# A GLA/S5 decoder step: norm temporaries in PSUM, sums of squares on VectorE, an earlier column sum

## The chip, the core and the metric

The kernel runs on one core of a Trainium2 chip. Its engines are called PE (TensorE, the matrix array; PEld is its weight load), DVE (VectorE), ACT (ScalarE), POOL (GpSimd) and SP (SyncE, which here issues the DMAs). Each runs its own queue in order, and semaphores make one wait for another. Operands lie in SBUF; PE writes PSUM, which has eight banks of 128x512 fp32 and which DVE and ACT can read and write too. The metric is the device time of one execution in microseconds (us).

## What is computed

Two layers of a decoder over 512 prompt tokens and 32 sample tokens with 1024 features: gated linear attention (GLA) and its MLP, then an S5 state-space mixer with a gated output (GLU) and its MLP. Each of the four sub-layers is wrapped in two root-mean-square norms, and the change concerns those around the sub-layers:

```python
def _rmsnorm(x, g):
    xf = x.astype(jnp.float32)
    y = xf * lax.rsqrt(jnp.mean(xf * xf, axis=-1, keepdims=True) + EPS)
    return (y * g.astype(jnp.float32)).astype(x.dtype)
...
    for i in range(DEPTH):
        h = _rmsnorm(x, prm['g_pre_mix'][i])
        ...                                # m = GLA or S5 mixer of h
        x = x + _rmsnorm(m, prm['g_post_mix'][i])
        h = _rmsnorm(x, prm['g_pre_mlp'][i])
        f = jnp.square(jax.nn.relu(h @ prm['w_up'][i])) @ prm['w_down'][i]
        x = x + _rmsnorm(f, prm['g_post_mlp'][i])
```

## The kernel before

**Tiles and jobs.** Features lie on the partitions, in `KD` = 8 blocks of 128; the 544 tokens lie along the free dimension in two halves, hf 0 of 288 and hf 1 of 256 (`HALF`). Each fp32 matmul is made of three: activations and weights are split into a high part (`xh`, `wh`, type fp32r) and what is left (`xl`, `wl`). A *job* is one 128-wide tile of outputs for one half: 8 blocks times 3 matmuls into one PSUM bank (`job`, `advance`), then `finish` copies it out (the "evac"). `PLAN` lists the jobs: groups of 4 or of 8 weight tiles, first all their jobs of half 0, then of half 1. The S5 input has an order of its own: five jobs of half 0, five of half 1, then in turn.

**Order.** There is no scheduler: instructions stand on each queue as the Python code emits them. `finish` runs, after job j's copy-out, the functions in `after[j]`; `defer(n, f)` appends f to the list n jobs ahead; `before_evac[j]` runs just ahead of job j's copy-out. `split_w` puts the weight split of later tiles between jobs: ACT casts `wh` (L113), DVE or POOL subtracts to get `wl` (L118, L120). While `dve_win` is 0, which `post` sets around the norms, POOL makes all of `wl`.

**The norms around a boundary.** At the end of a sub-layer the tiles of its output `acc` are finished one by one. `m_done` squares each on ACT into `sq` and adds it on DVE into `S1[hf]`. After the eighth, `post` defers: one job later `start` asks PE for the column sum of `S1` (a matmul with ones, `col_sums`, L243) and takes the root `r` (`rsqrt`: ACT makes an approximate root y, L251, and a scaled copy v of the sum, L252; DVE refines y in three instructions, L253 to L255). Then `step`, a few jobs in a row, walks the eight blocks: DVE scales `acc` by g and r (L318), adds it to the residual `X` (L320) and, for the next sub-layer, `xh` = X times its g (`pre_hi`: L278 on DVE for half 0, L280 on ACT for half 1), the square on ACT, its add into `S2[hf]` on POOL (L264 is the line of all these adds), and `xl` on DVE (`pre_lo`, L290). The first jobs of the next sub-layer need `xh` and `xl`; the copy-out of its first job needs `pre_scale`: the column sum of `S2`, and a root from it, `rs`. The last norm of the kernel is `last_done`. `SL` is the number of jobs over which each half's steps go.

Where the next sub-layer starts with a group of 8 tiles, half 1's eight jobs lie between half 0's last job and half 0's next one. So PE meets, in this order: those eight jobs; the next sub-layer's first job (it needs all of half 0's `xh` and `xl`); the column sum of `S2[0]`; the column sum of `S1[1]`, asked for by half 1's `start`; the second job.

**Banks.** PSUM's banks are two pools of four, `ps` and `held`. While `apart` is false, every request (`bank`) takes from the two in turn, so that jobs and small sums share all eight; while it is true, jobs take from `held` and everything else from `ps`. Before, it is true only from within the S5 input to the first third of the GLU.

Of the kernel before, what the change touches and what calls it, by code (L numbers as in the profile page):

```python
# [46 lines left out]
SL = (4,6)  # L47
# [25 lines left out]
class Builder:  # L73
    def __init__(self, tc, io):
        self.tc, self.nc, self.io = tc, tc.nc, io
        self.jobs = 0
        self.after = defaultdict(list)
        self.before_evac = defaultdict(list)
        self.hold, self.held = set(), []
# [166 lines left out]
    def rsqrt(self, ps, n, scale, out):  # L246
        nc = self.nc
        y = self.p_t.tile([128, 288], F32, tag="ny", name="ny", bufs=1)
        a = self.p_t.tile([128, 288], F32, tag="na", name="na", bufs=1)
        v, y, a = out, y[:, :n], a[:, :n]  # L250
        nc.scalar.activation(y, ps, AF.Abs_reciprocal_sqrt, scale=scale, bias=self.vec[:, V_EPS:V_EPS + 1])  # L251
        nc.scalar.activation(v, ps, AF.Copy, scale=scale, bias=EPS)  # L252
        nc.vector.tensor_mul(a, y, y)  # L253
        nc.vector.scalar_tensor_tensor(a, a, -0.5, v, op0=OP.mult, op1=OP.mult)
        nc.vector.scalar_tensor_tensor(out, a, 1.5, y, op0=OP.add, op1=OP.mult)  # L255

    def square_into(self, s, src, n, first, eng=None, later=False):
        nc = self.nc
        if first:
            nc.scalar.activation(s, src, AF.Square)  # L260
            return
        q = self.p_t.tile([128, 288], F32, tag="sq", name="sq", bufs=5)
        nc.scalar.activation(q[:, :n], src, AF.Square)
        add = lambda: (eng or nc.gpsimd).tensor_tensor(s, s, q[:, :n], op=OP.add)  # L264
        if later:
            self.defer(1, add)
        else:
            add()

    def pre_hi(self, hf, k, g, on_dve=False, later=False, squares=None):  # L270
# [30 lines left out]
    def post(self, hf, g_post, g_pre, sink=None):  # L301
# [10 lines left out]

        def step(ks):
            new = [k for k in ks if k < KD]
            xs, ms = ([t[:, k, c0:c1] for k in new] for t in (self.X, self.acc))
            for k, m in zip(new, ms):
                gk = self.vec[:, g_post + k:g_post + k + 1]
                nc.vector.scalar_tensor_tensor(m, m, gk, R["r"][:, :n], op0=OP.mult, op1=OP.mult)  # L318
            for x, m in zip(xs, ms):
                nc.vector.tensor_add(x, x, m)  # L320
            if g_pre is not None and ks[0]:
                self.pre_lo(hf, ks[0] - 1, g_pre)
            for k in new:
                if g_pre is not None:
                    self.pre_hi(hf, k, g_pre, hf == 0, True)
                if sink:
# [10 lines left out]
        self.defer(lead, start)  # L337
# [4 lines left out]
        ks = list(range(KD + 1))  # L342
# [49 lines left out]
    def m_done(self, m, hf, g_post, g_next, sink=None):  # L392
# [8 lines left out]
        if m == KD - 1:  # L401
            self.post(hf, g_post, g_next, sink)
# [181 lines left out]
    def gla_out(self, og):  # L584
        nc = self.nc

        def out_evac(m, hf, ps):
            c0, c1 = HALF[hf]
            nc.scalar.activation(self.acc[:, m, c0:c1], ps, AF.Copy)
            self.m_done(m, hf, V_POST, V_MPRE)  # L590
        self.run_block(og["h"], og["l"], out_evac)
# [516 lines left out]
    def s5(self, ctx):  # L1108
# [202 lines left out]
        OB = 6  # L1311
        self.after[self.jobs + OB].append(lambda: setattr(self, 'apart', True))
# [23 lines left out]
    def glu(self, zh, zl):  # L1336
# [15 lines left out]
        for q in (0, 4, 8):  # L1352
            self.run_block(zh, zl, lambda i, hf, ps: glu(i, q, hf, ps))
            if q == 0:
                self.apart = False


    def run(self):
        nc, tc, io = self.nc, self.tc, self.io
        ctx = ExitStack()  # L1360
        with ctx:
# [9 lines left out]
            self.vec = p.tile([128, V_END], F32, name="vec")  # L1371
            self.X = p.tile([128, KD, NT], F32, name="X")
# [156 lines left out]
```

## Time and profile before

| | |
|---|---|
| median of 3 runs | 1358.02 us (1356.08 to 1359.86) |
| the profiled execution | 1359.06 us, its span 1357.3 us |
| granted PE clock, mean | 0.978 |
| busy: PE / PEld / DVE / ACT / POOL | 1298.1 / 1270.3 / 798.9 / 602.4 / 509.9 us |
| HBM | 128.17 MB read, 25.46 MB written |

The span is from the first to the last instruction on the chip; the time of an execution is 1.8 us longer. Rows of the profile name instructions by line, engine, operation and tiles as out<-in, with partitions x elements; for groups there follow the total and the mean of one in ns. In square brackets stands the engine's idle time ahead of an instruction, and what ended it. `mm` and `held` are banks of jobs. Matmuls overlap in the array, so that one shows as longer than its distance to the next.

### The profile page before, as it was taken

Reading aid. Unit: us, or ns where it says so; the run is one execution under the profiler, and the core shown is the slowest. Engines: PE = TensorE matmul, PEld = TensorE weight load, DVE = VectorE, ACT = ScalarE, POOL = GpSimd, SP = SyncE. Lnnn points to the kernel's source line nnn. Section 1 sums busy time; section 2 is a strip of 40 time slices with the busy share of each in tenths; the row PEclk is TensorE's granted clock in tenths of the full one; section 3 lists DMA queues with packets and bytes.
Section 4 is the critical chain, followed back from the end, with each engine's and each line's share of the span. In section 5 each row is a group of like instructions: output and inputs, shape, how many; then the busy total and the mean of one; then the engine's idle time right before and its main releaser. Section 6 shows DMA issues by size and latency. Waiting matters only on the chain. (4 is left out here: it accounts for less than half of the span.)

```text
span 1357.3 us, 25681 instructions
## 1 busy us (share of the span) xinstructions
PE 1298.1 (96%) x9966; PEld 1270.3 (94%) x9966; DVE 798.9 (59%) x1779; ACT 602.4 (44%) x1349; POOL 509.9 (38%) x644
## 2 busy tenths in 40 slices
PE   7999999979999999999998988999899999999996
PEld 6899999979999999999997988999899999999996
DVE  7866564688535767666468689456841332332346
ACT  6633354645435646555434222434643432432432
POOL 4443244564381111121435443544633333343341
PEclk9999899999999999999998989999899999999998
DMA  6233222322325555544315687341222323222221
GB/s 190 94 128 102 104 68 86 121 65 75 98 71 161 174 162 172 164 149 152 109 47 187 176 254 222 96 125 35 91 78 74 99 79 109 78 81 91 78 63 67
DMA packets 80683, 155.31 MB, mean 114 GB/s; under 512 B 9040, under 2 KB 45264, under 8 KB 79536
## 3 DMA queue, kind: packets, MB, share of 16 engines
q1 hardware_dynamic: 80560, 153.66, 36.3%
q8 instruction: 78, 1.28, 0.4%
q14 instruction: 45, 0.37, 0.1%
HBM read 128.17 MB, written 25.46 MB: 113 GB/s over the span
## 5 line engine op out<-in xcount | busy, mean ns | idle before, releaser
L120 POOL TENSOR_TENSOR wl<-raw,wh 128x384 fp32r<-128x384 f32 (+3 forms) x351 | 351.9, 1014 | 597.8 <-ACT wh L113 588.9
L113 ACT ACTIVATE wh<-raw 128x512 fp32r<-128x512 f32 x368 | 219.6, 621 | 125.9 <-PE held L191 76.4
L118 DVE TENSOR_TENSOR wl<-raw,wh 128x128 fp32r<-128x128 f32 (+3 forms) x324 | 180.4, 568 | 102.6 <-ACT wh L113 96.6
L191 PE MATMUL held<-xh,wh 128*128 128x256 f32 (+1 forms) x792 | 235.1, 297 | 0.1
L191 PE MATMUL held<-xl,wh 128*128 128x256 f32 (+1 forms) x792 | 232.2, 293 | 0.8 <-DVE xl L290 0.8
L191 PE MATMUL held<-xh,wl 128*128 128x256 f32 (+1 forms) x792 | 230.9, 292 | 0.0
L191 PE MATMUL mm<-xl,wh 128*128 128x288 f32 (+1 forms) x744 | 216.7, 291 | 1.8 <-DVE xl L290 1.8
L191 PE MATMUL mm<-xh,wh 128*128 128x288 f32 (+1 forms) x744 | 218.2, 293 | 0.0
L191 PE MATMUL mm<-xh,wl 128*128 128x288 f32 (+1 forms) x744 | 215.1, 289 | 0.0
L191 PEld LDWEIGHTS held<-xh,wh 128*128 128x128 f32 x792 | 152.5, 193 | 1.6 <-issue 0.8
L191 PEld LDWEIGHTS held<-xl,wh 128*128 128x128 f32 x792 | 152.3, 192 | 1.4 <-DVE xl L290 1.0
L191 PEld LDWEIGHTS held<-xh,wl 128*128 128x128 f32 x792 | 152.0, 192 | 0.0
L191 PE MATMUL mm<-hh,wl 128*128 128x256 f32 (+1 forms) x512 | 147.5, 288 | 0.7 <-DVE wl L118 0.7
L191 PE MATMUL mm<-hl,wh 128*128 128x256 f32 (+1 forms) x512 | 148.1, 289 | 0.0
L191 PE MATMUL mm<-hh,wh 128*128 128x256 f32 (+1 forms) x512 | 148.1, 289 | 0.0
L191 PE MATMUL held<-hl,wh 128*128 128x256 f32 (+1 forms) x512 | 148.1, 289 | 0.0
L191 PE MATMUL held<-hh,wh 128*128 128x256 f32 (+1 forms) x512 | 148.0, 289 | 0.0
L191 PE MATMUL held<-hh,wl 128*128 128x256 f32 (+1 forms) x512 | 147.4, 288 | 0.0
L191 PEld LDWEIGHTS mm<-xl,wh 128*128 128x128 f32 x744 | 141.7, 190 | 3.2 <-DVE xl L290 3.0
L191 PEld LDWEIGHTS mm<-xh,wh 128*128 128x128 f32 x744 | 142.0, 191 | 1.3 <-issue 0.6
L191 PEld LDWEIGHTS mm<-xh,wl 128*128 128x128 f32 x744 | 141.3, 190 | 0.0
L363 ACT ACTIVATE r<-r 128x256 f32<-128x256 f32 (+1 forms) x128 | 55.0, 429 | 172.0 <-DVE r L361 171.9
(401 smaller groups left out, 2729.2 us busy)
## 6 DMA issues: line engine op xcount, KB each, us to landing
raw<-in_w SPq DMA_DIRECT2D x184, 512.0 KB, 3.6
S<-in_h SPq DMA_DIRECT2D x4, 1024.0 KB, 5.0
out_gla_s<-S SPq DMA_DIRECT2D x4, 1024.0 KB, 3.9
wd<-blk SPq DMA_DIRECT2D x16, 256.0 KB, 2.7
wd<-cs SPq DMA_DIRECT2D x16, 256.0 KB, 3.8
qd<-blk SPq DMA_DIRECT2D x16, 256.0 KB, 2.7
qt<-qd SPq DMA_DIRECT2D x16, 256.0 KB, 3.9
wt<-wd SPq DMA_DIRECT2D x12, 256.0 KB, 4.3
```

The costliest lines, as they stand in the source:

```text
L113: nc.scalar.activation(h[:, a:c], r[:, a:c], AF.Copy)
L118: nc.vector.tensor_sub(l[:, a:b], r[:, a:b], f32(h[:, a:b]))
L120: nc.gpsimd.tensor_sub(l[:, b:c], r[:, b:c], f32(h[:, b:c]))
L191: self.nc.tensor.matmul(ps[:, :c1 - c0], a[:, k], b[:, k, c0:c1], start=(k == 0 and i == 0), stop=(k == KD - 1 and i == 2))
L363: nc.scalar.activation(r[:, :n], r[:, :n], AF.Square)
```

## The change

- In `job`, functions in a new table `mid` are emitted ahead of a job's last block (the last 3 of its 24 matmuls). `post` puts half 0's `start` there, in the job behind the last one; half 1's stays behind that job.
- `m_done` issues, behind the last square, an ACT instruction of one column with the root's function (`spare`), so that its table is loaded there.
- `rsqrt`: y lies in a PSUM bank, and the first two DVE instructions change places of y and v, so that each of the three has one operand in PSUM.
- `step`: the product acc g r goes into a PSUM bank (`xm`) instead of back into `acc`; `xh` is always made on ACT; the square of X goes into the same bank. `xl` of a step's blocks follows in the next step, the last in a step of its own. The eight blocks go over 5 jobs instead of 4 for half 0 (`SL`), 6 as before for half 1; at the S5 input there are only 4.
- `square_into`: squares go into banks (`sq`), all adds are on DVE, and deferred ones are put at the head of the next job's list, so that they come before its step, the youngest first.
- `apart` is true from `gla_out` to the end.

```diff
-SL = (4,6)
+SL = (5,6)
...
+        if self.jobs in self.mid:
+            self.advance(t, hf, hi, lo, KD - 1)
+            for f in self.mid.pop(self.jobs):
+                f()
         self.advance(t, hf, hi, lo, KD)
...
     def rsqrt(self, ps, n, scale, out):
-        y = self.p_t.tile([128, 288], F32, tag="ny", name="ny", bufs=1)
+        y = self.bank("ny") if self.apart else self.p_t.tile([128, 288], F32, tag="ny", name="ny", bufs=1)
...
-        nc.vector.tensor_mul(a, y, y)
-        nc.vector.scalar_tensor_tensor(a, a, -0.5, v, op0=OP.mult, op1=OP.mult)
+        nc.vector.tensor_mul(a, y, v)
+        nc.vector.scalar_tensor_tensor(a, a, -0.5, y, op0=OP.mult, op1=OP.mult)
         nc.vector.scalar_tensor_tensor(out, a, 1.5, y, op0=OP.add, op1=OP.mult)
...
+        if q is None:
+            q = self.squares(n)
+        nc.scalar.activation(q, src, AF.Square)
+        add = lambda: (nc.vector if self.apart else eng or nc.gpsimd).tensor_tensor(s, s, q, op=OP.add)
         if later:
-            self.defer(1, add)
+            self.after[self.jobs + 1].insert(0, add)
...
+    def squares(self, n):
+        if self.apart:
+            return self.bank("sq")[:, :n]
+        return self.p_t.tile([128, 288], F32, tag="sq", name="sq", bufs=5)[:, :n]
...
         def step(ks):
+            ms = [self.bank("xm")[:, :n] for k in ks]
+            for k, m in zip(ks, ms):
                 gk = self.vec[:, g_post + k:g_post + k + 1]
-                nc.vector.scalar_tensor_tensor(m, m, gk, R["r"][:, :n], op0=OP.mult, op1=OP.mult)
+                nc.vector.scalar_tensor_tensor(m, self.acc[:, k, c0:c1], gk, R["r"][:, :n], op0=OP.mult, op1=OP.mult)
+            for k, m in zip(ks, ms):
+                x = self.X[:, k, c0:c1]
                 nc.vector.tensor_add(x, x, m)
+            if g_pre is not None:
+                for k in fresh:
+                    self.pre_lo(hf, k, g_pre)
+                fresh[:] = ks
+                for k, m in zip(ks, ms):
+                    self.pre_hi(hf, k, g_pre, False, True, None, m)
...
-        self.defer(lead, start)
+        if hf:
+            self.defer(lead, start)
+        else:
+            self.mid[self.jobs + 1].append(start)
...
-            part = ks[i * 9 // slots:(i + 1) * 9 // slots]
+            part = list(range(KD))[i * KD // slots:(i + 1) * KD // slots]
             self.defer(lead + i, lambda part=part: step(part))
+        self.defer(lead + slots, lambda: step([]))
...
         if m == KD - 1:
+            self.nc.scalar.activation(self.spare, self.vec[:, V_EPS:V_EPS + 1], AF.Abs_reciprocal_sqrt)
             self.post(hf, g_post, g_next, sink)
...
+        self.apart = True
         self.run_block(og["h"], og["l"], out_evac)
...
-        OB = 6
-        self.after[self.jobs + OB].append(lambda: setattr(self, 'apart', True))
...
-            if q == 0:
-                self.apart = False
```

How this moves the queues is shown at three places. Tile numbers shift by one (`S_80` and `S_81` before, `S1` of the two halves, are `S_81` and `S_82` now; `S_83` now is `S2` of half 0, `S_84` of half 1), and lines move by up to 18 (L318 is L330 now, L320 L333, L290 L301, L264 L270).

ACT at the end of gla_out's first half, from the last block's copy and square, before:

```order
L589 ACTIVATE acc<-mm 128x288
L263 ACTIVATE sq<-acc 128x288
L113 ACTIVATE wh<-raw 128x512
L589 ACTIVATE acc<-held 128x256
L260 ACTIVATE S_81<-acc 128x256
L251 ACT_TABLE_LOAD
```

and now:

```order
L606 ACTIVATE acc<-held 128x288
L269 ACTIVATE sq<-acc 128x288
L418 ACT_TABLE_LOAD
L418 ACTIVATE spare<-vec 128x1
L114 ACTIVATE wh<-raw 128x512
L256 ACTIVATE ny<-sums,vec 128x288
L257 ACTIVATE rp<-sums 128x288
L606 ACTIVATE acc<-held 128x256
L265 ACTIVATE S_82<-acc 128x256
```

The table load moved behind the square, and the root ahead of the next job's copy and square.

DVE at the same boundary, from the last instruction of the root, before:

```order
L255 SCALAR_TENSOR_TENSOR rp<-na,ny 128x288
L318 SCALAR_TENSOR_TENSOR acc<-acc,vec,rp 128x288 x2
L320 TENSOR_TENSOR X<-X,acc 128x288 x2
L278 TENSOR_SCALAR xh<-X,vec 128x288 x2
L290 SCALAR_TENSOR_TENSOR xl<-X,vec,xh 128x288
L318 SCALAR_TENSOR_TENSOR acc<-acc,vec,rp 128x288 x2
L320 TENSOR_TENSOR X<-X,acc 128x288 x2
L290 SCALAR_TENSOR_TENSOR xl<-X,vec,xh 128x288
```

and now:

```order
L260 SCALAR_TENSOR_TENSOR rp<-na,ny 128x288
L330 SCALAR_TENSOR_TENSOR xm<-acc,vec,rp 128x288
L333 TENSOR_TENSOR X<-X,xm 128x288
L330 SCALAR_TENSOR_TENSOR xm<-acc,vec,rp 128x288 x2
L333 TENSOR_TENSOR X<-X,xm 128x288 x2
L301 SCALAR_TENSOR_TENSOR xl<-X,vec,xh 128x288
L270 TENSOR_TENSOR S_83<-S_83,xm 128x288 x2
L270 TENSOR_TENSOR S_82<-S_82,sq 128x256
L330 SCALAR_TENSOR_TENSOR xm<-acc,vec,rp 128x288
L333 TENSOR_TENSOR X<-X,xm 128x288
L301 SCALAR_TENSOR_TENSOR xl<-X,vec,xh 128x288 x2
```

`xh` has left the queue, and the adds of the squares, of which S2's were on POOL and six of S1's stood behind all steps, stand between the steps.

DVE at the S5 input, half 1, from the last step to the root of the first job of half 1 (`us` is the copy-out of the fifth job of half 0), before:

```order
L318 SCALAR_TENSOR_TENSOR acc<-acc,vec,rp 128x256 x2
L320 TENSOR_TENSOR X<-X,acc 128x256 x2
L290 SCALAR_TENSOR_TENSOR xl<-X,vec,xh 128x256 x3
L1168 TENSOR_TENSOR us<-held,rs_84 128x72x4
L253 TENSOR_TENSOR na<-ny 128x256
```

and now:

```order
L330 SCALAR_TENSOR_TENSOR xm<-acc,vec,rp 128x256 x2
L333 TENSOR_TENSOR X<-X,xm 128x256 x2
L301 SCALAR_TENSOR_TENSOR xl<-X,vec,xh 128x256 x2
L1186 TENSOR_TENSOR us<-held,rs_85 128x72x4
L270 TENSOR_TENSOR S_84<-S_84,xm 128x256 x2
L301 SCALAR_TENSOR_TENSOR xl<-X,vec,xh 128x256 x2
L258 TENSOR_TENSOR na<-ny,rs_86 128x256
```

The last two `xl` moved behind the copy-out of the fifth job, with two adds ahead of them.

More of the change, by code (lines that the diff above doesn't have):

```diff
@@ L78, in __init__ @@
         self.before_evac = defaultdict(list)
+        self.mid = defaultdict(list)
         self.hold, self.held = set(), []
@@ L252, in rsqrt, with square_into @@
         nc.scalar.activation(v, ps, AF.Copy, scale=scale, bias=EPS)
-        nc.vector.tensor_mul(a, y, y)
-        nc.vector.scalar_tensor_tensor(a, a, -0.5, v, op0=OP.mult, op1=OP.mult)
+        nc.vector.tensor_mul(a, y, v)
+        nc.vector.scalar_tensor_tensor(a, a, -0.5, y, op0=OP.mult, op1=OP.mult)
         nc.vector.scalar_tensor_tensor(out, a, 1.5, y, op0=OP.add, op1=OP.mult)
-    def square_into(self, s, src, n, first, eng=None, later=False):
+    def square_into(self, s, src, n, first, eng=None, later=False, q=None):
         nc = self.nc
@@ L261, in square_into, with pre_hi @@
             return
-        q = self.p_t.tile([128, 288], F32, tag="sq", name="sq", bufs=5)
-        nc.scalar.activation(q[:, :n], src, AF.Square)
-        add = lambda: (eng or nc.gpsimd).tensor_tensor(s, s, q[:, :n], op=OP.add)
+        if q is None:
+            q = self.squares(n)
+        nc.scalar.activation(q, src, AF.Square)
+        add = lambda: (nc.vector if self.apart else eng or nc.gpsimd).tensor_tensor(s, s, q, op=OP.add)
         if later:
-            self.defer(1, add)
+            self.after[self.jobs + 1].insert(0, add)
         else:
             add()
-    def pre_hi(self, hf, k, g, on_dve=False, later=False, squares=None):
+    def squares(self, n):
+        if self.apart:
+            return self.bank("sq")[:, :n]
+        return self.p_t.tile([128, 288], F32, tag="sq", name="sq", bufs=5)[:, :n]
+    def pre_hi(self, hf, k, g, on_dve=False, later=False, squares=None, q=None):
         nc = self.nc
@@ L281, in pre_hi @@
         if squares is None:
-            self.square_into(self.S2[hf][:, :n], x, n, k == 0, None, later)
+            self.square_into(self.S2[hf][:, :n], x, n, k == 0, None, later, q)
         else:
-            q = self.p_t.tile([128, 288], F32, tag="sq", name="sq", bufs=5)[:, :n]
+            q = self.squares(n)
             nc.scalar.activation(q, x, AF.Square)
@@ L311, in start @@
             R["r"] = r
+        fresh = []
         def step(ks):
-            new = [k for k in ks if k < KD]
-            xs, ms = ([t[:, k, c0:c1] for k in new] for t in (self.X, self.acc))
-            for k, m in zip(new, ms):
+            ms = [self.bank("xm")[:, :n] for k in ks]
+            for k, m in zip(ks, ms):
                 gk = self.vec[:, g_post + k:g_post + k + 1]
-                nc.vector.scalar_tensor_tensor(m, m, gk, R["r"][:, :n], op0=OP.mult, op1=OP.mult)
-            for x, m in zip(xs, ms):
+                nc.vector.scalar_tensor_tensor(m, self.acc[:, k, c0:c1], gk, R["r"][:, :n], op0=OP.mult, op1=OP.mult)
+            for k, m in zip(ks, ms):
+                x = self.X[:, k, c0:c1]
                 nc.vector.tensor_add(x, x, m)
[L321 to L326, printed above, removed]
+            if g_pre is not None:
[4 more added lines that the diff above has]
+                    self.pre_hi(hf, k, g_pre, False, True, None, m)
+            if sink:
+                for k in ks:
                     sink(hf, k)
-            if g_pre is not None:
-                for k in ks[1:]:
-                    self.pre_lo(hf, k - 1, g_pre)
         at = self.wjob - 1
@@ L341, in post @@
         slots = min(gap - 1 - lead, SL[hf])
-        ks = list(range(KD + 1))
         for i in range(slots):
-            part = ks[i * 9 // slots:(i + 1) * 9 // slots]
+            part = list(range(KD))[i * KD // slots:(i + 1) * KD // slots]
             self.defer(lead + i, lambda part=part: step(part))
+        self.defer(lead + slots, lambda: step([]))
         if g_pre is not None:
@@ L1371, in run @@
             self.vec = p.tile([128, V_END], F32, name="vec")
+            self.spare = p.tile([128, 1], F32, name="spare")
             self.X = p.tile([128, KD, NT], F32, name="X")
```

## The prediction

> **What bounds the kernel now.** I read the page first, then the waits of TensorE in order of total time, then the stretches around the long waits with the granted clock, and last the instructions of the other engines there.
>
> ```profile
> span 1357.3 us, 25681 instructions
> PE 1298.1 (96%) x9966; PEld 1270.3 (94%) x9966; DVE 798.9 (59%) x1779; ACT 602.4 (44%) x1349; POOL 509.9 (38%) x644
> ```
>
> TensorE is busy nearly throughout, so only what it idles, or runs at a lowered clock, can be won. Its waits (us in total, times, longest) name the sums of squares:
>
> ```profile
> PE sums L243 <- DVE S L264: 9.0, 2, 5.2
> PE held L243 <- DVE S L264: 4.4, 1, 4.4
> PE held L243 <- POOL S L264: 4.4, 6, 1.1
> PE sums L243 <- POOL S L264: 1.1, 1, 1.1
> PE mm L191 <- DVE xl L290: 1.8, 4, 0.8
> PE held L191 <- DVE xl L290: 0.8, 1, 0.8
> ```
>
> They add to 21.5 us, and all but one of about 1 us near the start stand at three places: gla_out to MLP 0 (call it A), MLP 0 to the S5 input (B), GLU to MLP 1 (C). The stretches at A, B and C (columns: length, busy time of PE, PEld, DVE, ACT, POOL, then the granted clock):
>
> ```profile
> 293.10:296.30 3.20, 3.05 (x24) 2.82 (x22) 3.20 (x7) 2.73 (x7) 1.38 (x2) 1.00 0.00 0
> 296.30:304.90 8.60, 1.85 (x6) 1.10 (x7) 8.15 (x8) 4.69 (x12) 8.52 (x8) 0.74 0.41 122
> 304.90:309.40 4.50, 4.50 (x26) 4.41 (x25) 2.80 (x6) 1.52 (x4) 0.41 (x1) 0.73 0.42 119
> 715.00:723.20 8.20, 1.97 (x7) 1.19 (x7) 7.68 (x12) 4.32 (x10) 7.31 (x7) 0.83 0.38 99
> 723.20:728.40 5.20, 5.20 (x27) 5.11 (x26) 4.78 (x11) 0.87 (x3) 0.38 (x1) 0.62 0.91 327
> 947.70:955.60 7.90, 2.31 (x9) 1.29 (x9) 5.40 (x6) 4.34 (x11) 7.82 (x7) 0.80 0.38 109
> 955.60:960.60 5.00, 5.00 (x26) 4.91 (x25) 2.06 (x4) 2.82 (x7) 1.66 (x2) 0.63 0.39 145
> ```
>
> In each the array does 2 us of work in about 8, and the job behind it runs at 0.62 to 0.73 of the clock: (1 - 0.73) x 4.5 + (1 - 0.62) x 5.2 + (1 - 0.63) x 5.0 = 5.0 us more. The stalls at A, one by one, and what VectorE and GpSimd do meanwhile:
>
> ```profile
> 298.33 0.75 PE L243 MATMUL held<-S,cst 128*128 128x288 f32 x2 [1.06 <-POOL S L264]
> 304.33 1.19 PE L243 MATMUL sums<-S,cst 128*128 128x256 f32 x2 [5.25 <-DVE S L264]
> ...
> 296.62 7.57 DVE L264 TENSOR_TENSOR S<-S,sq 128x256 f32<-128x256 f32 x6
> ...
> 298.24 7.07 POOL L120 TENSOR_TENSOR wl<-raw,wh 128x512 fp32r<-128x512 f32 x5
> ```
>
> Six adds take 7.57 us, 1.26 each, beside GpSimd's weight halves of 1.4. Over the whole stretch of A (269.8 to 304.9) the means of VectorE's groups in ns are:
>
> ```profile
> L318 DVE SCALAR_TENSOR_TENSOR acc<-acc,vec,rp 128x288 f32<-128x288 f32 x8 | 8.0, 1036 | 0.0
> L264 DVE TENSOR_TENSOR S<-S,sq 128x256 f32<-128x256 f32 x7 | 7.5, 1075 | 0.5
> L320 DVE TENSOR_TENSOR X<-X,acc 128x288 f32<-128x288 f32 x8 | 5.1, 677 | 0.0
> L290 DVE SCALAR_TENSOR_TENSOR xl<-X,vec,xh 128x288 fp32r<-128x288 f32 x8 | 5.0, 635 | 0.0
> L278 DVE TENSOR_SCALAR xh<-X,vec 128x288 fp32r<-128x288 f32 x8 | 2.6, 359 | 0.0
> ```
>
> Over the whole run, a group with an operand in a PSUM bank, and ScalarE's weight casts:
>
> ```profile
> L361 DVE SCALAR_TENSOR_TENSOR r<-held,rs 128x288 f32<-128x288 f32 x33 | 15.0, 454 | 23.5 <-PE held L191 23.5
> ...
> L113 ACT ACTIVATE wh<-raw 128x512 fp32r<-128x512 f32 x368 | 219.6, 621 | 125.9 <-PE held L191 76.4
> ```
>
> So what limits A to C is VectorE's queue, stretched by GpSimd where both inputs are in SBUF: the operand in PSUM holds 0.45 us everywhere.
>
> **The change part by part.** I follow the queue orders from the moment at which the last block of the first half is copied out, with these rows for the start:
>
> ```profile
> 270.04 0.41 ACT L589 ACTIVATE acc<-mm 128x288 f32<-128x288 f32 x1 [1.76 <-PE mm L191]
> 273.75 1.28 ACT L251 ACT_TABLE_LOAD   x1
> 275.04 0.50 ACT L251 ACTIVATE ny<-sums,vec 128x288 f32<-128x288 f32 x1
> 275.44 0.40 ACT L252 ACTIVATE rp<-sums 128x288 f32<-128x288 f32 x1
> 275.57 0.46 DVE L253 TENSOR_TENSOR na<-ny 128x288 f32<-128x288 f32 x1 [4.15 <-ACT ny L251]
> 277.13 0.95 DVE L318 SCALAR_TENSOR_TENSOR acc<-acc,vec,rp 128x288 f32<-128x288 f32 x2
> ...
> 311.02 0.51 ACT L280 ACTIVATE xh<-X,vec 128x256 fp32r<-128x256 f32 x1 [2.19 <-DVE X L320]
> ```
>
> Earlier sum, earlier table. Root to first step, before: 277.13 - 270.04 = 7.1. Now the table (1.28) loads right behind the last square, and the column sum stands three matmuls earlier (0.4) and ahead of the job's own copy and square (0.8). The new root multiplies y by v, so it waits for the copy of 0.40 too, 0.3 later. 7.1 - 1.3 - 0.4 - 0.8 + 0.3 = 4.9, and a weight cast of 0.6 now lies in front: about 5.3.
>
> The steps. In pitches, blocks of one step cost VectorE 0.43 each for the scaling, 0.37 for the add to X, 0.43 for xl. xh moves to ScalarE (0.4, against 0.36 on VectorE); with the square (0.4) two blocks take 1.65 there. The S2 adds come from GpSimd to VectorE (0.45 each), and they stand ahead of the next step, the youngest first: VectorE waits for ScalarE's last square. That is a new wait; behind it queue the S1 add, the next scaling and all xl. A weight cast on ScalarE directly behind that square starts a GpSimd half of 1.3, which blocks the next scaling for 0.55 to 1.0 (both its inputs stay in SBUF).
> At A, from the copy: step 1 begins at 5.3 + 0.9 = 6.2; its two blocks take 1.6, ScalarE 2.2 (with the job's copy and square ahead), three adds 1.3: 11.3. Step 2, one block: 0.6 blocked + 0.9 + 0.9 + 0.9 = 3.3: 14.6. Step 3: 0.9 + 1.6 + 1.65 + 1.3 = 5.4: 20.0. Step 4: 0.5 + 1.6 + 1.45 + 1.35 = 4.9: 24.9. The last two xl, each blocked once, 2.8: 27.7, where the job that reads them wants them at 25.5. Three S1 adds 1.3: 29.0, sums 0.45: the second job behind starts at 29.45. Before: 304.9 - 270.0 = 34.9. Gain 5.5; the stall itself was 8.60 - 1.85 = 6.75. At B VectorE also copies the jobs out, which at A ScalarE does: the same walk ends 1.05 later, and it ended 0.5 earlier before: gain 3.9. At C each second job goes through a sigmoid, whose table has to come back (1.28), and a product (0.4 each) ahead of its square: 2.6 later, 0.8 earlier before: gain 2.1. Together 11.5.
>
> Clock. Of the 5.0 us, part stays, since stalls of 3 to 5 us are left. A shorter wait has already lowered it:
>
> ```profile
> 797.40 0.85 PE L1242 MATMUL yp<-area,qt 128*128 128x136 f32 x5 [1.98 <-DVE area L1224]
> ...
> 798.80:802.20 3.40, 3.40 (x18) 3.40 (x17) 2.57 (x8) 1.40 (x5) 2.12 (x3) 0.51 0.89 257
> ```
>
> One such stretch of 3.4 us at 0.51, partly over idle time, is 1.0 at each place: 3.0 stays, 2.0 is won. [...]
>
> The second half. Its chain starts when the first stall ends, so a shorter stall starts it later against the jobs. VectorE takes 7 S2 adds (2.8) and loses about as much of GpSimd's blocking. At A about 1 us more stall, at C 0.6 less. At B the next block comes after five jobs, and the order now puts the last two xl behind the copy-out of the fifth:
>
> ```profile
> 737.73 2.27 DVE L290 SCALAR_TENSOR_TENSOR xl<-X,vec,xh 128x256 fp32r<-128x256 f32 x3
> 739.92 0.68 DVE L1168 TENSOR_TENSOR us<-held,rs 128x288 f32<-128x288 f32 x1
> ...
> 741.45 0.70 PE L243 MATMUL held<-S,cst 128*128 128x256 f32 x2 [0.49 <-POOL S L264]
> ```
>
> The xl ended at 740.0, 2.0 behind the fifth job. Add 0.7 for the copy-out, 0.9 for adds and 1.25 for the later start: 4.9, where the job wants them at 2.6. So 2.3 of stall for 0.49: 1.8 lost. Sum of the second halves: -2.2.
>
> Banks. From gla_out to the end the jobs have four banks, where they had eight in turn with the rest. Almost everywhere a job is copied out long before the fourth job behind it. Not here, where ScalarE waits for GpSimd's S5 tables: the job that began at 382.92 is copied out at
>
> ```profile
> 397.37 0.39 ACT L371 ACTIVATE acc<-held 128x288 f32<-128x288 f32 x1
> ...
> 396.01 0.28 PE L191 MATMUL held<-hh,wh 128*128 128x256 f32 x1
> ```
>
> while the fourth job behind begins at 396.01: a new stall of 397.76 - 396.01 = 1.8, and at even odds a clock stretch of 1.7 (0.8). In gla_out's own first jobs 0.3 more. The last root of the kernel, which nothing covers, waits 0.3 longer for v. Together -3.2.
>
> Sum: 11.5 + 2.0 - 2.2 - 3.2 = 8.1 us. The profiled execution took 1359.06 us (span 1357.3), 1.0 above the median of 1358.02; 1358.0 - 8.1 gives 1350.
>
> Unknown prices. No instruction of VectorE or ScalarE writes PSUM in the trace. The nearest rows read it (454 ns) or leave it (L253, 0.46 us): no difference, and I take none. Ends: 0.05 less each, as ScalarE's copies out of PSUM are shorter than its squares in SBUF (0.41 against 0.45), or as much again as the instruction, 0.45 more. The scaling keeps two SBUF inputs and only its output moves; I take it as blocked like L318, whose free length is 0.51 and mean here 1036 ns. [...] Were it free instead, 1.9 us at each place, 5.6 in all, would come on top and give 1344; no row here has such an output.
>
> **The rivals.**
> (1) The stalls of the first half go altogether: if VectorE's waits for squares are filled, or the scaling is not blocked, the second job at A starts at 26.9 after the copy (the job ahead ends at 296.3, that is 26.3, and two sums of 0.3) rather than 29.45, 8.0 earlier than now. For it: GpSimd's adds and 1036 against 510 ns are gone. Against: my queue has 1.6 us of waiting in each step of two blocks. Three times 7.7 (8.0 at A, 7.7 and 7.4 by the starts at B and C) + 5.0 - 2.2 - 3.2 = 22.7: 1335.
> (2) The wait for ScalarE takes the place of the blocking in full: the chain from step 1 to the last add stays as long as now, the earlier start (1.8 each) goes into banks and second halves: 1357, no change. For it: 44% busy ScalarE has casts, copies and squares in one queue; against: 7.57 us for six adds cannot come back when they read PSUM.
> (3) Slower: writing PSUM is dear on VectorE. Eight scalings in each of six chains are on the path, 48 writes; at 0.17 us more each the gain of 8.1 is eaten, from 0.25 on the kernel is measurably slower, at 0.45 it is 48 x 0.45 - 8.1 = 13 slower: about 1368 to 1371, less what ScalarE's waits would hide, so 1364.
> (4) The waits that are left come in pieces under 2 us and lower the clock nowhere: 2.0 at A and B and the 0.8 at the banks more: 1347. For it: the xl come one by one. Against: the 1.98 us above. [...]
>
> **How the numbers follow.** Forecast (1346 to 1354) 0.45, (1) 0.13, (2) 0.20, (3) 0.12, (4) 0.10. What a measurement can tell from no change is 0.3%, 4.1 us. Faster: 0.45 + 0.13 + 0.10 = 0.68; same 0.20; slower 0.12. The range 1338 to 1360 leaves out most of (1) below and most of (3) above.
>
> **What would show it.** The adds to S at 0.42 to 0.46 us even beside GpSimd; the wait of 5.25, 4.43 and 3.75 us for the column sum cut to under 2, with xl waits of 1 to 4 us at A and C in front; at B a wait for xl of about 2 us after the fifth job of the S5 input; a wait of 1.8 us for a copy-out near 390; scalings of 1 us still. It is wrong if VectorE's instructions into PSUM are longer than 0.6 us without GpSimd, or if no wait for xl is left at all.

## The result and the profile after

The changed kernel takes 1342.37 us (median of 6 runs, 1341.47 to 1350.33) beside 1358.43 us of the kernel before on the same chip: a ratio of 0.990, 95% interval 0.9878 to 0.9922. Timed once more later it gave 0.9915 (0.9893 to 0.9937). So it is faster by 0.8 to 1.0%, about 11 to 16 us. Predicted were 1350, that is 8 us, with 1346 to 1354 as the forecast: both medians lie a little below it, and inside the range of 1338 to 1360.

The first lines of the page of after, and TensorE's waits (us in total, times, longest), to be held against those of before:

```profile
span 1344.0 us, 25691 instructions
PE 1290.9 (96%) x9966; PEld 1263.5 (94%) x9966; DVE 770.2 (57%) x1797; ACT 611.8 (46%) x1380; POOL 468.1 (35%) x602
...
PE held L196 <- DVE xl L301: 11.0, 10, 3.2
...
PE sums L248 <- DVE S L270: 2.3, 3, 1.5
...
PE held L248 <- POOL S L270: 1.3, 1, 1.3
PE held L196 <- ACT acc L386: 1.1, 1, 1.1
```

GpSimd lost 42 instructions and 42 us of work, and VectorE got 18 instructions more, yet worked 29 us less. The waits for sums of squares fell from 18.9 us to 3.6, of which the 1.3 near the start are the old ones; waits for `xl` rose from 2.6 to 11.0. VectorE's groups over the stretch of A (265.5 to 294.3; mean ns of one ahead of the last bar, then its idle time and what ended it) show why:

```profile
L330 DVE SCALAR_TENSOR_TENSOR xm<-acc,vec,rp 128x288 f32<-128x288 f32 x8 | 6.0, 776 | 0.0
L301 DVE SCALAR_TENSOR_TENSOR xl<-X,vec,xh 128x288 fp32r<-128x288 f32 x8 | 5.4, 709 | 0.0
L333 DVE TENSOR_TENSOR X<-X,xm 128x288 f32<-128x288 f32 x8 | 3.3, 446 | 0.1
L270 DVE TENSOR_TENSOR S<-S,xm 128x288 f32<-128x288 f32 x7 | 3.2, 455 | 3.1 <-ACT xm L269 3.0
L270 DVE TENSOR_TENSOR S<-S,sq 128x256 f32<-128x256 f32 x7 | 2.9, 415 | 0.1
```

The adds, each with an operand in PSUM, hold 415 to 455 ns: 14 adds of squares take 6.1 us, where 7 took 7.5. Those that keep both inputs in SBUF (`xm`, `xl`) are still stretched, 776 and 709 ns in the mean against 0.53 us at 270.84 and 0.50 at 282.48, where GpSimd rested, and VectorE now waits 3.0 us for ScalarE's squares. The same places in the row of stretches (length, busy time of PE, PEld, DVE, ACT, POOL, granted clock):

```profile
291.66:294.30 2.64, 1.69 (x8) 1.19 (x9) 1.87 (x5) 2.48 (x7) 2.64 (x3) 1.00 0.49 119
294.30:299.00 4.70, 4.70 (x38) 4.70 (x37) 2.83 (x7) 1.53 (x4) 1.58 (x2) 1.00 0.54 160
704.18:707.10 2.92, 1.10 (x6) 0.64 (x5) 2.14 (x6) 2.25 (x7) 1.24 (x2) 1.00 0.59 202
707.10:712.00 4.90, 4.90 (x36) 4.85 (x37) 4.30 (x10) 1.04 (x3) 1.28 (x2) 1.00 0.90 258
932.04:941.10 9.06, 4.01 (x14) 2.60 (x14) 7.24 (x12) 5.31 (x13) 4.08 (x3) 0.78 0.35 115
941.10:946.00 4.90, 4.90 (x26) 4.72 (x27) 1.82 (x4) 2.77 (x7) 2.53 (x2) 0.72 0.20 69
```

At A and B the array idles 1.0 and 1.8 us where it idled 6.8 and 6.2, and the clock stays at 1.00. At C it still idles 5.1 (5.6 before), with the clock down as before.

To say where the time went, the distance between copy-outs of the same jobs was taken from the traces. A1 goes from gla_out's last block of half 0 to the third job of MLP 0, A2 from there to the fourth copy-out of its first down group; T from there to a job behind the S5 tables (copied out at 475.5 us in before); B1 from the seventh job of MLP 0's last group to the third of the S5 input, B2 from there to its ninth; C1 from GLU's last copy of half 0 to the third job of MLP 1, C2 from there to the seventh copy-out of its first down group. Two profiles of each kernel agree within 0.2 us in every column:

| us | A1 | A2 | T | B1 | B2 | C1 | C2 |
|---|---|---|---|---|---|---|---|
| before (2 profiles) | 47.4 | 47.9 | 110.2 | 46.9 | 18.2 | 51.2 | 56.5 |
| after (2 profiles) | 39.0 | 49.7 | 110.5 | 41.3 | 20.3 | 50.4 | 58.3 |
| difference | -8.4 | +1.8 | +0.3 | -5.6 | +2.0 | -0.8 | +1.8 |

Together -8.9 us; what stands between these stretches is equal within 0.2, but for the GLA stage and the S5 mixer, which differ from run to run of one kernel as well (first experiment).

### The profile page after: what moved, and what is told of

Same layout as the page of the kernel before. It is cut to its first block, busy times and chain, and to the rows that moved or that the text cites. A ratio compares the mean times of both kernels' runs of the same rounds, so it can differ in the third digit from the quotient of the medians.

```text
span 1344.0 us, 25691 instructions
## 1 busy us (share of the span) xinstructions
PE 1290.9 (96%) x9966; PEld 1263.5 (94%) x9966; DVE 770.2 (57%) x1797; ACT 611.8 (46%) x1380; POOL 468.1 (35%) x602
## 4 chain that ended last, share of the span: by engine, by line
PE 73%; DVE 12%; ACT 5%; DMA 3%; POOL 3%; issue 2%; SPq 2%; DVEq 0%; ACTq 0%; POOLq 0%
PE held L196 60%; PE mm L196 4%; DVE xm L330 2%; DVE S L270 1%; PE yp L1260 1%; DVE xl L301 1%; PE kp L1076 1%; ACT xh L291 1%; ACT wh L114 1%; DVE X L333 1%; ACT xm L269 1%; PE held L778 1%; PE os L778 1%; DMA wt<-wd 0%; DVE na L259 0%
## 5 line engine op out<-in xcount | busy, mean ns | idle before, releaser
L196 PE MATMUL held<-xl,wh 128*128 128x256 f32 (+1 forms) x1344 | 391.3, 291 | 11.0 <-DVE xl L301 11.0
L196 PE MATMUL held<-xh,wh 128*128 128x256 f32 (+1 forms) x1344 | 393.4, 293 | 0.1
L196 PE MATMUL held<-xh,wl 128*128 128x256 f32 (+1 forms) x1344 | 388.1, 289 | 0.0
L196 PE MATMUL held<-hh,wh 128*128 128x256 f32 (+1 forms) x1024 | 296.2, 289 | 1.1 <-ACT acc L386 1.1
L196 PE MATMUL held<-hl,wh 128*128 128x256 f32 (+1 forms) x1024 | 296.1, 289 | 0.0
L196 PE MATMUL held<-hh,wl 128*128 128x256 f32 (+1 forms) x1024 | 294.7, 288 | 0.0
L196 PEld LDWEIGHTS held<-xh,wh 128*128 128x128 f32 x1344 | 255.2, 190 | 2.6 <-issue 1.2
L196 PEld LDWEIGHTS held<-hh,wh 128*128 128x128 f32 x1024 | 193.2, 189 | 3.0 <-ACT acc L386 1.3
L196 PEld LDWEIGHTS held<-hl,wh 128*128 128x128 f32 x1024 | 193.0, 188 | 0.1
L196 PEld LDWEIGHTS held<-hh,wl 128*128 128x128 f32 x1024 | 192.6, 188 | 0.0
```

The source lines that it names most:

```text
L196: self.nc.tensor.matmul(ps[:, :c1 - c0], a[:, k], b[:, k, c0:c1], start=(k == 0 and i == 0), stop=(k == KD - 1 and i == 2))
```

## The experiments

All were timed beside the kernel before; ratios are to it.

**Both kernels again.** No edit.

> The changed kernel once more, unaltered, for its spread and for the place of its lowered-clock stretches. Theory (the clock is granted on a fixed grid of 3.41 us whose place against the program differs from run to run, so a gap of 1.5 to 3 us costs a half-clock stretch in one run and none in the next): median again 1341 to 1346 us, single runs spread over some 5 to 9 us, and the last og low part of the GLA stage (249.4 us in the first profile, 253.9 in the kernel before) lies anywhere from 249 to 254 though nothing in that stage differs. Rival (the new order of the three root instructions makes the GLA stage 4.5 us shorter): 249.4 within 0.5, with half-clock stretches again at about 53, 107.6 and 189.5 us.

> The kernel before once more, for a second profile. Theory (the grid's place is chance): its last og low part of the GLA stage comes at 250 to 254 us, not always 253.9, with another set of half-clock stretches than the six at 61.6, 68.4, 109.4, 146.9, 153.7 and 194.7. Rival (the root's order decides): 253.9 within 0.5 and six such stretches again. In both, the stalls of 5.25, 4.43 and 3.75 us for the column sum stay within 0.5.

Measured: 1345.72 us (1344.59 to 1351.87), ratio 0.9915; the kernel before, over 23 runs on that chip, 1357.3 (1352.27 to 1363.18). The copy-out at which the GLA stage's differences end, in before, before again, after, after again:

```profile
270.04 0.41 ACT L589 ACTIVATE acc<-mm 128x288 f32<-128x288 f32 x1 [1.76 <-PE mm L191]
```
```profile
268.51 0.41 ACT L589 ACTIVATE acc<-mm 128x288 f32<-128x288 f32 x1 [1.79 <-PE mm L191]
```
```profile
265.56 0.41 ACT L606 ACTIVATE acc<-held 128x288 f32<-128x288 f32 x1 [1.79 <-PE held L196]
```
```profile
269.08 0.41 ACT L606 ACTIVATE acc<-held 128x288 f32<-128x288 f32 x1 [1.79 <-PE held L196]
```

The changed kernel was 4.5 us ahead here in its first profile and came 0.6 behind the kernel before's second in its own second. So these 4.5 us of the first comparison of traces are not the change; the rival falls. In the second profile of before the column-sum waits were 5.25, 3.85 and 3.18: the first as expected, the others 0.6 less, with half-clock stretches lying otherwise (B1 and C1 are equal within 0.02). What was measured of those stretches stands in the last section.

**The earlier start alone**, on the kernel before:

```diff
+        if self.jobs in self.mid:
+            self.advance(t, hf, hi, lo, KD - 1)
+            for f in self.mid.pop(self.jobs):
+                f()
...
-        self.defer(lead, start)
+        if hf:
+            self.defer(lead, start)
+        else:
+            self.mid[self.jobs + 1].append(start)
...
+            self.nc.scalar.activation(self.spare, self.vec[:, V_EPS:V_EPS + 1], AF.Abs_reciprocal_sqrt)
```

> The kernel before with the earlier start alone: the first half's column sum ahead of the last three matmuls of the next job, and the root's table loaded behind the last square; temporaries, adds, xh and banks as before. Theory (the start is one of two parts, 1.8 us at each of A, B and C, of which what GpSimd's blocking does not eat again comes through): 1352 to 1356, with S adds of 1.0 to 1.3 us and column-sum waits of 2.5 to 4 us left. Rival (the start is all of the gain): 1342 to 1346. Rival (the start is eaten by the queues behind it): 1357 to 1360.

Ratio 0.9984 (0.9967 to 1.0001), 1355.0 us: in the theory's range, but the interval just reaches no change. A1 is 46.1 and B1 45.8, that is 1.3 and 1.1 less than before, C1 51.1; the seven stretches together are 2.7 less. The waits for the sums are all there, longer than the theory's 2.5 to 4 us:

```profile
PE sums L248 <- DVE S L269: 6.8, 2, 5.2
PE held L248 <- POOL S L269: 6.0, 5, 2.8
PE held L248 <- DVE S L269: 4.4, 1, 4.4
```

Neither rival: about half of the three times 1.8 us comes through. The seven adds at A still take 1077 ns each (1075 before), and behind them the rest is lost.

**All temporaries in SBUF**, on the changed kernel:

```diff
-        y = self.bank("ny") if self.apart else self.p_t.tile([128, 288], F32, tag="ny", name="ny", bufs=1)
+        y = self.p_t.tile([128, 288], F32, tag="ny", name="ny", bufs=1)
...
-        if self.apart:
-            return self.bank("sq")[:, :n]
...
-            ms = [self.bank("xm")[:, :n] for k in ks]
+            ms = [self.acc[:, k, c0:c1] for k in ks]
...
-                    self.pre_hi(hf, k, g_pre, False, True, None, m)
+                    self.pre_hi(hf, k, g_pre, False, True)
```

> The changed kernel with its temporaries back in SBUF: squares, the root's y and acc g r (in place in acc); the order of all queues, the adds on VectorE and the early start stay. Theory (an operand in PSUM keeps VectorE's adds clear of GpSimd's weight halves): S adds beside those halves take 1.0 to 1.3 us again instead of 0.45, the adds to X too, so some 8 blocked instructions more at each of A, B and C, 5 us each at most, partly in waits that were there: 1348 to 1354. Rival (the order and the earlier start make the gain, PSUM none): 1341 to 1345.

Ratio 1.0027 (1.0012 to 1.0043), 1360.7 us: the whole gain is gone and more, beyond what the theory expected. Order, adds on VectorE and earlier start without PSUM make the kernel slower than before; the rival falls.

**The squares alone in SBUF**, with `xm` and `y` in PSUM (the edit above without its first and third parts):

> The changed kernel with all squares in SBUF tiles and their adds on VectorE as in it; acc g r and the root's y stay in PSUM. It parts the 15 us between the changed kernel (0.9915 of before) and the one with everything in SBUF (1.0027). Theory (the adds of the squares are what GpSimd stretched: 13 or 14 in each chain against 8 adds to X): they are blocked again and most of the gain is gone, 0.997 to 1.001 of before, 1353 to 1358. Rival (the adds to X, on which xh, the squares and xl wait, carry the gain): 0.990 to 0.994, 1344 to 1349.

Ratio 1.0000 (0.9983 to 1.0018). The theory's case; and its rows at A (269.1 to 303.0) narrow it further:

```profile
L270 DVE TENSOR_TENSOR S<-S,sq 128x256 f32<-128x256 f32 x7 | 8.2, 1165 | 0.1
...
L270 DVE TENSOR_TENSOR S<-S,sq 128x288 f32<-128x288 f32 x8 | 3.7, 458 | 5.6 <-ACT sq L269 5.4
L331 DVE TENSOR_TENSOR X<-X,xm 128x288 f32<-128x288 f32 x8 | 3.3, 446 | 0.1
```

Only the seven adds into `S1` of the other half are stretched, 1165 ns in the mean against 415; the eight of 288 (one of them `S1`'s own last) take 458, though both inputs are in SBUF. That each of these began while GpSimd rested is how I read it; these rows do not show it. With `xm` in SBUF too, the adds to X took 449; `xm` and `y` in PSUM are worth about 0.3% (1.0027 against 1.0000, intervals that overlap a little; the seven stretches differ by 3.9 us). So of what was put into PSUM, the squares of `acc` carry most of the gain by these rows: 7 x 0.75 = 5.2 us in VectorE's queue at A. A kernel with these squares alone in PSUM was not timed.

**The changed kernel without its earlier start** (the edit of `early` taken back):

> The changed kernel without its earlier start: the first half's column sum behind the next job again and no table load ahead; PSUM temporaries, adds and order stay. Theory (by the prediction the start is worth 1.8 us at each of A, B and C where nothing stands in between): 5 us longer than the changed kernel, 1348 to 1352, with xl waits in front up from 5 to about 10 us in total. Rival (the earlier start is eaten: alone on the kernel before it gave 0.16%): 1344 to 1347.

Ratio 0.9961 (0.9945 to 0.9976), 1352.15 us: the earlier start is worth 0.5% here, 6 to 8 us, the theory's size or a little more. A1 is 41.0 instead of 39.0, B1 43.3 instead of 41.3, C1 and C2 together 111.3 instead of 108.7. The `xl` waits rose only from 11.0 to 11.2 in total, though, not by 5; in the first halves of A and B they rose (0.7 to 2.4 and 0.4 to 1.9), in the second they fell (1.3 to none and 2.2 to 0.4). Alone the two parts give 0.2% and 0.4%, together about 0.9%. In the seven stretches the start is worth 2.7 us by itself and 5.0 beside the other parts, so it pays more once the adds behind it no longer stretch; the times point the same way, but their intervals hardly part.

**Who adds S2.** On the changed kernel, squares of X in SBUF tiles, their adds back on GpSimd:

```diff
-            q = self.squares(n)
+            q = self.squares(n) if eng else self.p_t.tile([128, 288], F32, tag="sq", name="sq", bufs=5)[:, :n]
...
-        add = lambda: (nc.vector if self.apart else eng or nc.gpsimd).tensor_tensor(s, s, q, op=OP.add)
+        add = lambda: (eng or nc.gpsimd).tensor_tensor(s, s, q, op=OP.add)
...
-                    self.pre_hi(hf, k, g_pre, False, True, None, m)
+                    self.pre_hi(hf, k, g_pre, False, True)
```

> The changed kernel with the squares of X in SBUF tiles and their adds into S2 back on GpSimd; acc g r, y and the squares of acc stay in PSUM, the adds into S1 on VectorE, and the order stays. [...] Rival (what counts is that VectorE's adds have an operand in PSUM, who adds S2 doesn't matter): 1343 to 1347, column-sum waits under 2 us.

Ratio 0.9876 (0.9854 to 0.9899), 1341.62 us, a little below the rival's. I had expected column-sum waits of 2 to 4 us back at A, B and C, and 1349 to 1354; that fell. GpSimd's adds at A take 958 ns each, behind weight halves, and TensorE waits for none of them at A, B or C. VectorE has 7 instructions less in each chain, 14 at each place, and at A it waits 1.8 us for ScalarE's squares instead of 3.0. GpSimd's adds, and TensorE's waits:

```profile
L270 POOL TENSOR_TENSOR S<-S,sq 128x288 f32<-128x288 f32 x7 | 6.7, 958 | 0.2
```
```profile
PE held L196 <- DVE xl L301: 5.2, 10, 1.9
PE held L196 <- ACT acc L386: 1.6, 1, 1.6
PE sums L248 <- DVE S L270: 0.4, 1, 0.4
```

A1 is 38.1, B1 38.6, C1 45.7. C2 is 1.2 longer, and so is T by 1.3, there by the wait of 1.6 for a copy-out. So moving S2's adds to VectorE is a part of the change that gains nothing; that GpSimd's adds were late in the kernel before (1.06 us of wait at each place) because the chain ahead of them was, fits this but was not tried.

**The last xl a job sooner**, **four jobs instead of five**, **both**:

```diff
-        self.defer(lead + slots, lambda: step([]))
+        self.defer(lead + slots - 1, lambda: step([]))
```
```diff
-SL = (5,6)
+SL = (4,6)
```

> The changed kernel with the xl of the last two blocks (half 0: of the last step's) in the same job as their step, ahead of the next job's copy-out, instead of a job later. Theory (the 11.0 us of xl waits that the changed kernel has left come from those last xl standing behind a copy-out and the adds): xl waits fall from 11 to 2 to 5 us in total, at the S5 input's second half to 0, at C's first half from 4.6 to about 1.5; two half-clock stretches less: 1336 to 1340. Rival (VectorE's queue is full there, and what is pulled ahead pushes the adds and so the column sum back as much): 1343 to 1347, the waits moved from xl to the column sums.

> The changed kernel with the first half's eight blocks over 4 jobs as before, not 5. Theory (at A and B VectorE's queue sets the pace, so nothing moves there; at C the jobs do, since each step waits behind a job's sigmoid and product, and a job fewer ends the chain some 3 us sooner): C's first xl waits fall from 4.6 to 1 to 2 us, A and B within 1 us: 1341 to 1344. Rival (five jobs were needed because four crowd ScalarE: VectorE waits for two squares in each step): A and B end 1 us later each, 1345 to 1349.

> Both: 4 jobs for the first half, and the last blocks' xl in the step's own job. Theory: the gains lie on the same wait at C and add elsewhere: 1335 to 1339, and all xl waits together under 4 us. Rival (queue full): 1343 to 1348.

Ratios 0.9869 (0.9846 to 0.9892), 0.9899 (0.9874 to 0.9923), 0.9885 (0.9861 to 0.9909). With the last `xl` sooner their waits are 2.2 us instead of 11.0, and the column sums get 7.8:

```profile
PE sums L248 <- DVE S L270: 7.8, 7, 2.0
PE held L196 <- DVE xl L301: 2.2, 2, 1.2
```

Both expectations hold in part: the wait moved, as the rival has it, but what moved is smaller, and B2 (18.6 instead of 20.3), B1 (39.7) and C1 (48.9) are shorter. Four jobs change nothing at C in sum: C1 is 1.4 shorter and C2 1.5 longer. The wait for `xl` at C turned into one for a bank, which no theory had:

```profile
PE held L196 <- ACT acc L1362: 2.8, 1, 2.8
```

So `tail` came out at its theory's time, 1339.5, without all of the theory's cause, and `four` at its theory's, 1343.5, with A1 and B1 0.3 longer, not 1. Both edits together miss: 1343.0 us, the rival's lower end, though the `xl` waits fell to 2.8 as the theory has it; column sums (5.0) and the bank (2.8) took their place.

**S2 on GpSimd and the last xl sooner**, the two edits that gained:

> The changed kernel with S2's adds on GpSimd (squares of X in SBUF) and the last xl of each half in the job of their step: the two edits that each gained. Theory (with VectorE relieved of 14 adds, the xl pulled ahead delay nothing that PE waits for): no column-sum wait over 0.5 us, xl waits in total 1 to 3 us, 0.982 to 0.986 of before, 1334 to 1339. Rival (they cure the same wait): as the kernel with GpSimd's adds alone, 0.9876, 1341 to 1344.

Ratio 0.9878 (0.9855 to 0.9901), 1341.23 us: the rival. What `xl` no longer waits for, the column sums wait for again, now GpSimd's adds (4.5 us in four waits) and once VectorE's (2.1). The three fastest kernels, 0.9869, 0.9876 and 0.9878, cannot be told apart. Their ratios are 0.2 to 0.5% below those of the changed kernel, but each interval overlaps one or both of its own, so that a further gain is not shown.

**Four banks alone**, on the kernel before:

```diff
+        self.apart = True
         self.run_block(og["h"], og["l"], out_evac)
...
-        self.after[self.jobs + OB].append(lambda: setattr(self, 'apart', True))
...
-            if q == 0:
-                self.apart = False
```

> The kernel before with four banks for the jobs from gla_out to the end, nothing else. The prediction put 1.8 us of wait and 0.8 of clock on the job that ScalarE copies out late behind the S5 tables; in the changed kernel that wait was 1.07, and 0.71 was there before. Theory (the tables come relatively earlier in the changed kernel because GpSimd has no S adds left; with those adds the predicted 1.8 is right): a copy-out wait of 1.6 to 2.0 us at 396, the stretch from the third MLP copy-out to the group behind it 1 to 1.5 us longer, the whole 1358 to 1361. Rival (the deep queue of banks was never needed): wait under 1.1, 1356 to 1358.

Ratio 1.0003 (0.9988 to 1.0019). The wait behind the S5 tables is the predicted one, 1.67 us, and T grew by 1.9.

```profile
PE held L191 <- DVE acc L373: 4.8, 2, 4.5
PE held L191 <- ACT acc L1345: 2.7, 1, 2.7
PE held L191 <- ACT acc L589: 2.2, 2, 2.0
PE held L191 <- ACT acc L371: 1.7, 1, 1.7
```

By the wait it is the theory's case; the time, 1358.08 us, lies where the theory's range and the rival's nearly meet. New waits for copy-outs of 2.0 at A and 2.7 at C cost nothing: they take the place of other waits ahead of the last add, which comes no later for them (A1 47.5, C1 51.3 as before). The one of 4.5 at B, for a copy-out that stands in VectorE's queue behind the chain, cost more: B1 is 0.4 longer, and B2 1.5. The stretches together are 3.9 longer, which the whole time, equal within 0.2%, does not show.

## Why the prediction was right

**What bounds the kernel, and the cure: right.** The adds of squares stretched by GpSimd were the limit, and an operand in PSUM freed them (0.9915 with the squares in PSUM, 1.0000 without). The measured adds are 0.41 to 0.46 us, as said. The seven of 256 columns at A took 415 ns in the mean with an operand in PSUM (after), 1165 with both inputs in SBUF (`xonly`).

**Earlier start: right.** 7.1 to 5.3 us after the copy was predicted; the first scaling stands at 270.84, 5.28 behind the copy at 265.56:

```profile
265.56 0.41 ACT L606 ACTIVATE acc<-held 128x288 f32<-128x288 f32 x1 [1.79 <-PE held L196]
...
266.44 1.28 ACT L418 ACT_TABLE_LOAD   x1
...
268.54 0.47 ACT L256 ACTIVATE ny<-sums,vec 128x288 f32<-128x288 f32 x1
```
```profile
270.84 0.53 DVE L330 SCALAR_TENSOR_TENSOR xm<-acc,vec,rp 128x288 f32<-128x288 f32 x1
```

**PSUM as dear or cheap as read: right.** `xm` free of GpSimd took 0.53 us (before 0.51), `ny` 0.47 (0.50), squares into PSUM 0.39. **The scaling stays blocked: right**, but by less, a mean of 776 ns against 1036. Where its output went made no difference here: 638 ns into SBUF (`sbuf`), 647 into PSUM (`xonly`). So the time came near the 1344 named for a free scaling without that cause.

**First halves: A and B under-rated, C mis-sized.** With their share of the clock (2.0 over three places) the steps gave A 6.2, B 4.6, C 2.8; measured 8.4, 5.6 and 0.8. At A the second job came 28.4 us behind the copy rather than 29.45, and no lowered clock was left, where I kept one stretch at each place. At C the step that failed is the walk through VectorE's queue, with "a product (0.4 each)" and the S2 adds in it:

```profile
932.49 0.93 DVE L301 SCALAR_TENSOR_TENSOR xl<-X,vec,xh 128x288 fp32r<-128x288 f32 x2
934.68 1.32 DVE L1366 TENSOR_TENSOR acc<-acc,s 128x256 f32<-128x256 f32 x1 [1.26 <-ACT s L1365]
935.93 0.93 DVE L270 TENSOR_TENSOR S<-S,xm 128x288 f32<-128x288 f32 x2
936.77 1.96 DVE L301 SCALAR_TENSOR_TENSOR xl<-X,vec,xh 128x288 fp32r<-128x288 f32 x2
```

The product has two SBUF inputs and took 1.32 where I put 0.4, and the queue waited 1.26 for its sigmoid; the last `xl` stand behind both and behind two S2 adds, and the array waited 3.20 for them, 4.6 in all. The product was priced too low from the start; over the stretch of C (921.2 to 955.6) the kernel before has for it:

```profile
L1350 DVE TENSOR_TENSOR acc<-acc,s 128x256 f32<-128x256 f32 x4 | 3.4, 853 | 2.5 <-ACT s L1349 2.5
```

But its price is not the whole: the wait of 3.2 us is the same in `late`, `xonly` and `sbuf`, and it is gone in `tail`, which pulls those `xl` ahead (C1 48.9; there the column sums wait 2.0 and 1.9), and in `pool`, which takes the S2 adds out of VectorE's queue (C1 45.7, 4.7 less). So what cost C its gain is mainly the place of the last `xl` behind adds and product; how the 2.0 us divide was not measured.

**Second halves: B right, C wrong in sign.** Predicted 1 lost at A, 1.8 at B, 0.6 won at C; measured 1.8, 2.0 and 1.8 lost. At B two waits make up the loss, and the second is the named one, behind the fifth job's copy-out (723.38 to 724.07). The first is for `xl` of the step before, ahead of that copy-out, and had not been foreseen, so that 2.0 beside 1.8 is partly luck. `tail`, which pulls the last `xl` ahead, took 1.7 us of B2 back; the first wait stayed, 1.16.

```profile
723.12 0.39 PE L196 MATMUL held<-xl,wh 128*128 128x256 f32 x1 [1.07 <-DVE xl L301]
725.23 0.44 PE L196 MATMUL held<-xl,wh 128*128 128x256 f32 x1 [1.09 <-DVE xl L301]
```

At C the array waits 0.49 and 1.48 us for `xl` in the second half, where it waited 0.17 before. Why it lost where I had put 0.6 won was not tried by itself.

**Banks: the mechanism right, the size too large.** 1.8 and 0.8 of clock were predicted, the wait was 1.07 and T grew by 0.3. On the kernel before the wait is 1.67 (`apart`), and 1.64 with GpSimd's adds back (`pool`). The S5 tables' first instruction moved from 355.70 to 341.97, 13.7 earlier, while the jobs there moved by 11.0 (copy-out 365.31 to 354.27): with no adds in its queue GpSimd reaches the tables sooner. The traces of the others agree: ahead of the same copy-out the tables start by 9.6 us in `apart`, with the long wait, by 12.3 to 12.6 in every kernel that has S2's adds on VectorE, and by 10.6 in `pool`, where adds and long wait are back. The kernel before already waited 0.71 there, which the predicted 1.8 left out. In after the clock was not lowered: with the wait of 1.07 the array was busy for 2.34 us of 384.08 to 387.49, and the granted clock was 1.00 there and up to 390.91. For the wait of 1.67 this is not shown.

**The rivals.** (1) did not occur: 11 us of `xl` waits were left. (2) occurred in part, VectorE's 3.0 us for squares at A, but did not eat the gain. (3) is out by the rows. (4), no lowered clock, held at A and at B's first half (1.00), not at B's second half (0.50 from 725.41 to 728.82) and at C (0.78 and 0.72).

**The sum.** The stretches come to 8.9 us; their terms were put at 8.7 (8.1, and 0.6 for gla_out's first jobs and the last root, which lie outside). The first halves of A and B brought 3.2 more, their second halves cost 1.0 more, the banks 2.3 less, and C brought 4.4 less. That these two agree is luck: the errors cancel. The medians differ by 11.6 and 16.1, 3 to 7 us more than the stretches. In the two profiles of each kernel the spans differ by 12.9 on average: 8.9 in the stretches, 2.0 up to gla_out's last copy-out of half 0, 2.3 in the S5 mixer (from B2's end to C1's start), and 0.2 lost behind C2. The 2.0 are not the change: over all 14 profiles that copy-out comes at 267.2 us on average in the four with the root as before, and at 267.4 in the other ten. The S5 mixer takes 167.6 and 166.5 in the same two groups, in a spread of 163.3 to 170.1; whether a part of it is the change stays open.

## What to carry to other kernels

Where VectorE and GpSimd work side by side, look for VectorE instructions with two SBUF inputs whose mean is two to three times that of their shape (here 1036 ns against 510, 1165 against 415), and put one input into PSUM where a producer such as ScalarE can write it there at no cost (squares of 256 columns took 389 ns into PSUM, 417 into SBUF). By the rows at A it is enough to do it for those that stand beside GpSimd's work; that is an estimate, not timed by itself. Taking the work from GpSimd was not needed here: with S2's adds left there the kernel was no slower. Starting a chain earlier and unblocking it were worth more together than apart here (the start 5.0 us beside the other parts, 2.7 by itself, over the seven stretches), so neither should be judged alone. Before two traces are compared stage by stage, profile the same kernel twice: here a stage that no part of the change was meant for moved by 4.5 us between two traces.

## What was not expected of the hardware

In before and after the recorded clock changes on a grid of 3.413 us (every change lies on it within 0.001 us), whose steps are called cells here, and the grid's place against the program is another in each run: its offset from the span's start is 0.12 us in before and 1.79 in after. Behind 200 us, 13 cells at full clock in these two traces have one at half clock behind them; the array was busy in each of the 13 for at most 1.47 of 3.41 us. Behind the other cells at full clock, in which it was busy for at least 1.77, the clock stays at 1.00. In after again a cell that was busy for 1.64 has one at half clock behind it. Two cells and those behind them, of after and of after again:

```profile
704.93:708.34 3.41, 1.94 (x12) 1.43 (x11) 2.27 (x6) 3.04 (x9) 2.48 (x2) 1.00 0.80 240
708.34:711.76 3.42, 3.42 (x28) 3.42 (x27) 3.18 (x9) 0.17 (x1) 0.04 (x1) 1.00 0.93 282
722.00:725.41 3.41, 1.25 (x8) 1.00 (x8) 3.38 (x10) 1.49 (x4) 0.27 (x4) 1.00 0.73 286
725.41:728.82 3.41, 3.41 (x15) 3.23 (x15) 0.75 (x3) 1.41 (x4) 0.07 (x1) 0.50 0.02 5
```
```profile
707.73:711.14 3.41, 1.77 (x8) 1.26 (x9) 2.31 (x7) 2.55 (x8) 1.91 (x2) 1.00 0.55 189
711.14:714.56 3.42, 3.42 (x28) 3.42 (x27) 3.14 (x8) 0.74 (x2) 0.61 (x1) 1.00 0.92 290
724.80:728.21 3.41, 1.64 (x12) 1.23 (x10) 3.38 (x10) 1.49 (x4) 0.27 (x4) 1.00 0.66 260
728.21:731.62 3.41, 3.06 (x12) 2.88 (x13) 0.69 (x2) 0.73 (x3) 0.00 (x0) 0.50 0.02 5
```

Busy for 1.94 and 1.77 of 3.41 us: the next cell keeps 1.00. Busy for 1.25 and 1.64: the next has 0.50, up to 1.7 us more for the same work. So whether idle time of about 2 us cost clock in these traces went with how much of it fell into one cell: 1.47 and 1.64 us did not, 2.16 and 1.77 did. Runs of one kernel spread over 4 to 11 us, and the clock went with it: of the 28 runs of the kernel before on one chip the fastest, 1352.77, has a mean granted clock of 0.983, the slowest, 1362.32, one of 0.976.

In the GLA stage, between 55 and 195 us, the busy share does not tell: before has six half-clock cells there and after two, each behind a cell that is shown as busy throughout. In this one of after, 16 matmuls of 4 columns stand for 1.95 us; what such matmuls count for stays open.

```profile
104.19:107.60 3.41, 3.41 (x29) 3.21 (x28) 2.86 (x10) 2.25 (x7) 1.12 (x3) 1.00 0.00 0
107.60:111.01 3.41, 3.41 (x16) 3.23 (x16) 1.39 (x4) 0.38 (x1) 0.54 (x1) 0.50 0.46 144
```

Two inputs in SBUF did not stretch an add by themselves: in before one of 288 columns, at 270.96, took 458 ns between two instructions of GpSimd (268.42 to 269.49, and from 271.53), while the six of 256 from 296.62 on, with GpSimd at work all along, took 1.26 us each. What mattered here is which instructions fall beside GpSimd's, and the order of the queues decides that.
